# A transformer trunk on one core: weight loads queued five chunks ahead, three quarters of the residual transposed by DMA, last stores on one queue

## The chip, the cores and the metric

The kernel runs on one core of a Trainium2 chip. The core has TensorE (matrix products), VectorE (DVE), ScalarE (ACT) and GpSimd (POOL) as computing engines, SyncE (SP), which here only issues DMAs, and 16 DMA engines that move data between HBM and the on-chip memory SBUF. TensorE writes to PSUM, a small accumulation memory. Each engine takes its instructions in order; semaphores order the engines among each other. The metric is the device time of one execution in microseconds, as the median of several runs. Before the change it is 821.35 us (three runs, 820.9 to 821.37).

## The reference, cut to what matters

A trunk of two pre-norm residual layers over 256 tokens of width 2048, in float32, and a last RMS norm:

```python
def reference(x, norm_g, final_g, w_in_even, w_out_even, rpb_b, w_in_odd, w_out_odd, sinks_c, qnorm_d, knorm_d):
    h = x
    for layer in range(DEPTH):              # 2
        y = rms_norm(h, norm_g[layer])
        if layer % 2 == 0:
            h = h + even_layer(y, w_in_even[i], w_out_even[i], rpb_b[i])
        else:
            h = h + odd_layer(y, w_in_odd[i], w_out_odd[i], sinks_c[i], qnorm_d[i], knorm_d[i])
    return rms_norm(h, final_g)
```

Each layer projects the normed input (2048 to 8192 columns in the even layer, fewer in the odd one), runs two groups of eight attention heads of width 128 on parts of the result, multiplies their outputs by a SiLU gate, and projects the 2048 columns back. The even layer has a dilated sliding-window group and a neighbourhood group with a learned position bias (`rpb_b`); the odd layer has windowed grouped-query attention with sinks and dense attention with normed and rotated queries and keys. The weights, some 140 MB, are used once each.

## The kernel before, in words

**Products in three parts.** Every float32 matrix is split into a high half (rounded to the type that TensorE multiplies fast, `F32R`) and a low half (the rest). A product is then high x high + high x low + low x high. `split` (L89) makes the halves of data: ACT casts or scales into `hi`, DVE subtracts into `lo`.

**Weights in chunks.** All weights come as 274 chunks of 128 x 1024 words (512 KB) in the order of the list `plan`. A `Weights` object (L54) loads a chunk into one of five `wraw` buffers through SP (L65, or `pinned` for the first eight), casts it into one of three `whi` buffers on ACT (L69) and subtracts into `wlo` on DVE (L70). `weights()` (L78) keeps three such objects made and hands out the oldest. So in the program's text the load stands just ahead of its cast; the planner of the framework, which orders each engine's instructions by a simulated time, may issue it earlier. `pinned` (L85) and `keep_in_program_order` tie an instruction behind the one that the program put before it on the same engine; what isn't tied may slip past others.

**The steps.** `by_feature` (L258) takes four chunks for 256 features (16 products a chunk), `by_token` (L277) eight chunks for 512 columns (12 products a chunk of 512 columns). After each chunk `step()` (L216) does one piece of the side work: one eviction of a finished accumulator (`evac`), one piece of `post`, and one piece of an attention (`bg`). An attention of two heads (`attend`, L406) goes through logits, probabilities, transposition, splits and the weighing of the values, a piece per chunk.

**The transposition in the attention** (L458 to L475) uses no TensorE: POOL copies the words of the probabilities into two planes of 16-bit halves (L463), two DMA transposes, `pinned` on SP through L87, turn them, and POOL joins the halves to words again (L474).

**The bias of a neighbourhood head** (`bias_rpb`, L388) is loaded by four small DMAs from a table in HBM into a single buffer `rpb`, and POOL subtracts it from a mask (L403). Two heads are loaded when a query projection is evicted, which occurs four times, in the third and fourth unit of the even layer.

**Between the layers.** `project_out("even", next_input)` multiplies the gated outputs (`mh`, `ml`) by the output weights for four blocks `n` of 512 columns of h: blocks 0 and 1 together in 16 chunks, then block 2 in 8, then block 3 in 8. When a block is complete, `add_h` (L539) adds it to h on DVE and `next_input` (L654) makes the odd layer's input of it: eight TensorE transposes against `ident` into PSUM (`ps_ht`, L660), four splits with the norm's gain (L95, L96), and the square sums for the norm on ACT.

**Start and end.** While the first eight chunks are multiplied, `opening(j)` loads the four blocks of x into h (`load_h`, for j = 4 to 7), for the square sums of the first norm. At the end, block 3 of the odd output is finished one token tile after the other: its last four weight chunks are made early, in the room of the input tiles X (`beside`, L755), and `finish` (L798) scales h on DVE or ACT and stores it through SP, two of the last six stores through ACT's queue (L806, L807).

Of the kernel before, what the change touches and what calls it, by code (L numbers as in the profile page):

```python
# [9 lines left out]
F32 = mybir.dt.float32  # L10
F32R = mybir.dt.float32r
# [7 lines left out]
P = 128  # L19
# [11 lines left out]
WARM = 15  # L31
AHEAD = 2
RPB_R, RPB_C = 15, 31


@with_exitstack
def encoder(ctx, tc, a, out):
# [3 lines left out]
    big = pool("big", 1)  # L41
    wp = pool("wp", 5)
    hp = pool("hp", 3)
# [10 lines left out]
    class Weights:  # L54


        def __init__(self, src, hi=None, lo=None, x=None):
            raw = wp.tile([P, 1024], F32, tag="wraw", name="wraw")
            self.hi = hi or hp.tile([P, 1024], F32R, tag="whi", name="whi")
            self.lo = lo or hp.tile([P, 1024], F32R, tag="wlo", name="wlo")  # L60
            cuts = KK if x in (0, 1) else 1
            cols = [slice(i * 1024 // cuts, (i + 1) * 1024 // cuts) for i in range(cuts)]
            for i, c in enumerate(cols):
                load = nc.sync.dma_start if x is None else pinned
                load(raw[:, c], src[:, c])  # L65
                if x is not None and i == 0:
                    pinned(xraw[x], a["xt"][x].rearrange("p (k t) -> p k t", k=KK))
            for i, c in enumerate(cols):
                nc.scalar.copy(self.hi[:, c], raw[:, c])  # L69
                nc.vector.tensor_sub(self.lo[:, c], raw[:, c], self.hi[:, c].bitcast(F32))  # L70
                if x is not None:
                    for m in (i,) if cuts > 1 else range(KK):
# [15 lines left out]

    def split(hi, lo, src, scale=None):  # L89

        if scale is None:
            nc.scalar.copy(hi, src)
# [123 lines left out]
    def step():  # L216

        advance(evac)
        advance(post)
        attention()  # L220

    def attention():
# [13 lines left out]
    def drain():  # L236
        while evac or post or bg:
            step()

    def need(pr):  # L240
# [310 lines left out]
    def out_plan(kind):  # L551
        plan.extend((a["w_out_" + kind][n][pr], None) for n, pr in out_order(kind))

# [6 lines left out]
    for u in range(4):  # L560
        for pr, kind in even_order(u):
            if kind == "v":
                plan.extend((a["even_t"][u][j], None if u else j) for j in range(8))
            else:
                plan.extend((a["even_f"][2 * u + pr]["qkg".index(kind)][j], None) for j in range(4))
    out_plan("even")
    for t, fs in ((0, ()), (1, (10, 11)), (2, (12, 13))):
        plan.extend((a["odd_t"][t][j], None) for j in range(8))
        plan.extend((a["odd_f"][f][j], None) for f in fs for j in range(4))
    plan.extend((a["odd_f"][f][j], None) for f in (0, 1, 2, 6, 3, 7, 4, 8, 5, 9) for j in range(4))  # L570
    out_plan("odd")
# [174 lines left out]
    def beside(n, i):  # L746
# [5 lines left out]
        if n == 2 and i % 2:  # L752
            j = i // 2
            room = X[j].rearrange("p k c t -> p (k c t)")
            final.append(Weights(a["w_out_odd"][NN - 1][late[j]], room[:, :1024], room[:, 1024:]))  # L755
        if (n, i) in ((2, 4), (2, 6), (3, 1)):
# [41 lines left out]
    def finish(n, t, r, cols=full, scalar=False):  # L798
# [8 lines left out]
        pin(queue.dma_start(out[t * P : (t + 1) * P, n * 512 + cols.start : n * 512 + cols.stop], y))  # L807

# [107 lines left out]
```

## Time and profile before

| | |
|---|---|
| median of three runs | 821.35 us |
| the profiled execution | 820.54 us, its span 818.8 us |
| TensorE (PE) busy | 808.6 us, 99% of the span |
| VectorE (DVE) / ScalarE (ACT) / GpSimd (POOL) busy | 576.1 / 447.3 / 110.6 us |
| moved by DMA | 166.91 MB, mean 204 GB/s |
| mean granted TensorE clock | 0.996 |

The span runs from the first to the last instruction of the profile. A row of a group gives line, engine, operation, output<-input, shape, count, then busy time in us, mean ns of one, and the idle time of the engine ahead of it with what ended it. A row of a timeline gives start and length in us. A row of who waited for whom gives total us, times, and the longest. A row of windows gives the window, its length, and the busy us of each engine with its instruction count in brackets, then the clock, the DMA engines' busy share and GB/s. SPq and ACTq are the issuing queues of SP and ACT.

### The profile page before, as it was taken

The numbers are of one execution on the slowest core, as the hardware profiler recorded it, in microseconds if no ns is written. First come the engines' busy times: TensorE is split into PE (matmuls) and PEld (weight loads), VectorE is DVE, ScalarE is ACT, GpSimd is POOL, SyncE is SP. The second block draws the span as 40 slices with busy tenths as digits, with TensorE's granted clock in tenths as the row PEclk, the third lists the DMA queues.
The fourth block names the chain that finished last, engine by engine and source line by source line (L and its number), as shares of the span: only waits on it lengthen the run. The fifth ranks groups of instructions, "written<-read, shape, count | busy, mean of one in ns | idle before, by whom it ended". The sixth has DMA issues, their size and how long they took to land.

```text
span 818.8 us, 11775 instructions
## 1 busy us (share of the span) xinstructions
PE 808.6 (99%) x4317; PEld 695.1 (85%) x4317; DVE 576.1 (70%) x856; ACT 447.3 (55%) x712; POOL 110.6 (14%) x88
## 2 busy tenths in 40 slices
PE   9999999999999999999999999999999999999995
PEld 7888888888888888888888888888899888888884
DVE  6677675677857886587655577685987777775763
ACT  7745454554545554455445544657666665664651
POOL 0002020021302140050200000002112222221000
PEclk9999999999999999999999999999999999999998
DMA  8956765575755766565654555556577775777532
GB/s 336 354 210 209 271 213 177 208 213 168 233 182 171 241 173 220 203 194 197 213 177 172 186 186 172 200 192 198 161 183 226 224 222 184 227 197 225 209 126 104
DMA packets 90682, 166.91 MB, mean 204 GB/s; under 512 B 48960, under 2 KB 50112, under 8 KB 90560
## 3 DMA queue, kind: packets, MB, share of 16 engines
q1 hardware_dynamic: 90192, 165.61, 62.5%
q8 instruction: 34, 0.56, 0.3%
q10 hardware_dynamic: 432, 0.54, 0.2%
q14 instruction: 24, 0.20, 0.1%
HBM read 155.64 MB, written 3.05 MB: 194 GB/s over the span
## 4 chain that ended last, share of the span: by engine, by line
PE 98%; DMA 0%; ACT 0%; DVE 0%; issue 0%; ACTq 0%; DVEq 0%
PE ps_f L267 34%; PE ps_f L271 17%; PE ps_t L102 14%; PE ps_t L103 14%; PE ps_t L104 14%; PE ps_s L103 1%; PE ps_s L104 1%; PE ps_s L102 1%; PE ps_out L103 1%; PE ps_out L102 1%; PE ps_out L104 1%; PE ps_ht L660 0%; DMA wraw<-in_even_t 0%; PE ps_tr L372 0%; ACT h L803 0%; ACT whi L69 0%
## 5 line engine op out<-in xcount | busy, mean ns | idle before, releaser
L70 DVE TENSOR_TENSOR wlo<-wraw,whi 128x1024 fp32r<-128x1024 f32 (+1 forms) x270 | 344.4, 1276 | 187.8 <-ACT whi L69 187.3
L69 ACT CAST whi<-wraw 128x1024 fp32r<-128x1024 f32 (+1 forms) x270 | 281.9, 1044 | 300.9 <-PE ps_t L104 130.7
L267 PE MATMUL ps_f<-x,whi 128*128 128x512 f32 x1184 | 372.3, 396 | 0.0
L271 PEld LDWEIGHTS ps_f<-x,wlo 128*128 128x128 f32 x1184 | 222.4, 188 | 52.9 <-DVE wlo L70 0.7
L271 PE MATMUL ps_f<-x,wlo 128*128 128x256 f32 x1184 | 233.0, 278 | 0.0
L267 PEld LDWEIGHTS ps_f<-x,whi 128*128 128x128 f32 x1184 | 180.9, 189 | 0.5
L102 PE MATMUL ps_t<-whi,x 128*128 128x512 f32 (+1 forms) x256 | 96.8, 381 | 0.3 <-ACT x L95 0.3
L103 PE MATMUL ps_t<-wlo,x 128*128 128x512 f32 (+1 forms) x256 | 96.4, 379 | 0.0
L104 PE MATMUL ps_t<-whi,x 128*128 128x512 f32 (+1 forms) x256 | 96.1, 377 | 0.0
L463 POOL COPY ph<-pr 128x1024 uint16<-128x1024 uint16 x32 | 39.5, 1233 | 418.1 <-ACT pr L453 252.0
L102 PE MATMUL ps_t<-whi,mh 128*128 128x512 f32 x240 | 93.8, 391 | 0.0
L103 PE MATMUL ps_t<-wlo,mh 128*128 128x512 f32 x240 | 93.7, 391 | 0.0
L104 PE MATMUL ps_t<-whi,ml 128*128 128x512 f32 x240 | 93.6, 390 | 0.0
L104 PEld LDWEIGHTS ps_t<-whi,x 128*128 128x128 f32 x256 | 48.5, 189 | 9.0
L102 PEld LDWEIGHTS ps_t<-whi,x 128*128 128x128 f32 x256 | 48.5, 189 | 9.0 <-ACT x L95 0.6
L474 POOL COPY pt<-pa 128x1024 uint16<-128x1024 uint16 x32 | 50.4, 1576 | 37.5 <-DMA pa<-ph 37.2
L103 PEld LDWEIGHTS ps_t<-wlo,x 128*128 128x128 f32 x256 | 48.6, 190 | 8.2
L104 PEld LDWEIGHTS ps_t<-whi,ml 128*128 128x128 f32 x240 | 45.1, 188 | 9.3
L103 PEld LDWEIGHTS ps_t<-wlo,mh 128*128 128x128 f32 x240 | 45.1, 188 | 8.9
L102 PEld LDWEIGHTS ps_t<-whi,mh 128*128 128x128 f32 x240 | 45.1, 188 | 8.9
L445 ACT ACTIVATE pr<-lg,mn 128x256 f32<-128x256 f32 (+1 forms) x48 | 24.0, 501 | 16.5 <-POOL ph L463 8.9
L403 POOL TENSOR_TENSOR bias<-maskB,rpb 128x512 f32<-128x512 f32 x8 | 12.5, 1567 | 138.5 <-DMA rpb<-rows 138.5
(129 smaller groups left out, 664.4 us busy)
## 6 DMA issues: line engine op xcount, KB each, us to landing
wraw<-in_even_f SPq DMA_DIRECT2D x96, 512.0 KB, 3.5
wraw<-in_odd_f SPq DMA_DIRECT2D x56, 512.0 KB, 3.7
wraw<-in_w_out_even SPq DMA_DIRECT2D x32, 512.0 KB, 3.3
wraw<-in_w_out_odd SPq DMA_DIRECT2D x32, 512.0 KB, 4.3
wraw<-in_even_t SPq DMA_DIRECT2D x30, 512.0 KB, 4.3
wraw<-in_odd_t SPq DMA_DIRECT2D x24, 512.0 KB, 3.2
xraw<-in_xt SPq DMA_DIRECT2D x8, 256.0 KB, 7.0
h<-in_x SPq DMA_DIRECT2D x4, 512.0 KB, 8.6
```

The lines of the kernel that those rows point to most:

```text
L69: nc.scalar.copy(self.hi[:, c], raw[:, c])
L70: nc.vector.tensor_sub(self.lo[:, c], raw[:, c], self.hi[:, c].bitcast(F32))
L102: nc.tensor.matmul(dst, lh, rh, start=first, stop=False, skip_group_check=True)
L103: nc.tensor.matmul(dst, lh, rl, start=False, stop=False, skip_group_check=True)
L104: nc.tensor.matmul(dst, ll, rh, start=False, stop=last, skip_group_check=True)
L267: nc.tensor.matmul(acc[:, f, :], w.hi[:, c], xx[k], start=k == 0, stop=False, skip_group_check=True)
L271: nc.tensor.matmul(acc[:, f, :S], w.lo[:, c], xh[k], start=False, stop=k == KC - 1, skip_group_check=True)
L403: nc.gpsimd.tensor_tensor(b, maskB.unsqueeze(1).to_broadcast([P, 2, S]), raw, op=ALU.subtract)
L445: nc.scalar.activation(p[:, t, :W], lg[:, t, :W], AF.Exp, bias=mn[:, t : t + 1], scale=-1.0, accum_out=den[:, t : t + 1],)
L463: nc.gpsimd.tensor_copy(halves, words)
L474: nc.gpsimd.tensor_copy(words.bitcast(U16).rearrange("p c (q s) -> p s c q", s=2), st[i])
```

## The change

- `Weights` is parted: the constructor only loads, always `pinned`; `prepare()` casts and subtracts. `load_ahead()` keeps up to five loaded chunks that aren't prepared, and is called before each preparation and once more before a chunk is handed out. The four early chunks of the last block come through the same plan, with the X tiles as their halves, and `beside` takes them by `weights()`.
- `load_h(n)` is called at j = 1 to 4.
- `next_input` no longer uses TensorE for blocks 0, 1 and 2. Per half block (`c`) a generator `turned_input` is queued in `turns`: POOL copy into 16-bit planes; two DMA transposes; an empty step; POOL copy back to words (in the single `rpb` buffer); two splits, whose ACT part is tied in program order; an empty step. `turning()`, called at the end of each `step()`, moves each generator on by one step, the next one only when the one before it has done three. Block 3 keeps the TensorE transposes.
- `finish` always stores through SP, and the order and cut of the last token tile's stores differ: block 0 in two halves, block 1, block 2, block 3 whole.

```diff
+RAW = 5
...
-    wp = pool("wp", 5)
+    wp = pool("wp", RAW)
...
         def __init__(self, src, hi=None, lo=None, x=None):
-            raw = wp.tile([P, 1024], F32, tag="wraw", name="wraw")
-            self.hi = hi or hp.tile([P, 1024], F32R, tag="whi", name="whi")
-            self.lo = lo or hp.tile([P, 1024], F32R, tag="wlo", name="wlo")
+            self.raw = wp.tile([P, 1024], F32, tag="wraw", name="wraw")
+            self.hi, self.lo, self.x = hi, lo, x
             cuts = KK if x in (0, 1) else 1
-            cols = [slice(i * 1024 // cuts, (i + 1) * 1024 // cuts) for i in range(cuts)]
-            for i, c in enumerate(cols):
-                load = nc.sync.dma_start if x is None else pinned
-                load(raw[:, c], src[:, c])
+            self.cols = [slice(i * 1024 // cuts, (i + 1) * 1024 // cuts) for i in range(cuts)]
+            for i, c in enumerate(self.cols):
+                pinned(self.raw[:, c], src[:, c])
                 if x is not None and i == 0:
                     pinned(xraw[x], a["xt"][x].rearrange("p (k t) -> p k t", k=KK))
-            for i, c in enumerate(cols):
+
+        def prepare(self):
+            raw, x = self.raw, self.x
+            if self.hi is None:
+                self.hi = hp.tile([P, 1024], F32R, tag="whi", name="whi")
+                self.lo = hp.tile([P, 1024], F32R, tag="wlo", name="wlo")
+            for i, c in enumerate(self.cols):
                 nc.scalar.copy(self.hi[:, c], raw[:, c])
...
-    plan, ready = [], []
-
-    def weights(ahead=AHEAD):
-
-        while plan and len(ready) <= ahead:
-            src, x = plan.pop(0)
-            ready.append(Weights(src, x=x))
+    plan, loaded, ready = [], [], []
+
+    def load_ahead():
+        while plan and len(loaded) < RAW:
+            loaded.append(Weights(*plan.pop(0)))
+
+    def weights():
+
+        while (plan or loaded) and len(ready) <= AHEAD:
+            load_ahead()
+            ready.append(loaded.pop(0))
+            ready[-1].prepare()
+        load_ahead()
         return ready.pop(0)
...
-    def split(hi, lo, src, scale=None):
+    def split(hi, lo, src, scale=None, kept=lambda x: x):
...
-            nc.scalar.mul(hi, src, scale)
+            kept(nc.scalar.mul(hi, src, scale))
...
     def step():
...
         attention()
+        turning()
...
+    turns = []
+
+    def turning():
+
+        for i, t in enumerate(list(turns)):
+            if i and steps[id(turns[i - 1])] < 3:
+                break
+            steps[id(t)] += 1
+            next(t)
+        if turns and steps[id(turns[0])] == 6:
+            turns.pop(0)
...
     def out_plan(kind):
-        plan.extend((a["w_out_" + kind][n][pr], None) for n, pr in out_order(kind))
+        for n, pr in out_order(kind):
+            plan.append((a["w_out_" + kind][n][pr],))
+            if (kind, n) == ("odd", 2) and pr in ORDER[kind][1::2]:
+                j = ORDER[kind].index(pr) // 2
+                room = X[j].rearrange("p k c t -> p (k c t)")
+                plan.append((a["w_out_odd"][NN - 1][ORDER[kind][4 + j]], room[:, :1024], room[:, 1024:]))
...
-        if j > 3:
-            load_h(j - 4)
+        if 0 < j < 5:
+            load_h(j - 1)
...
+    def turned_input(n, c):
+
+        halves = tp.tile([P, 2, 2, S], U16, tag="tmp2", name="hh")
+        across = tp.tile([P, 2, 2, S], U16, tag="pr", name="ha")
+        cols = h[n][:, :, c * S : (c + 1) * S].bitcast(U16)
+        nc.gpsimd.tensor_copy(halves, cols.rearrange("p t (k s) -> p t s k", s=2))
+        yield
+        for t in range(2):
+            pinned(
+                across[:, :, :, t * P : (t + 1) * P].rearrange("p s c q -> p (s c) q"),
+                halves[:, t].rearrange("p s k -> p (s k)"), transpose=True,
+            )
+        yield
+        yield
+        words = tp.tile([P, 2, S], F32, tag="rpb", name="hw", bufs=1)
+        nc.gpsimd.tensor_copy(words.bitcast(U16).rearrange("p c (q s) -> p s c q", s=2), across)
+        yield
+        for i in range(2):
+            k = 4 * n + 2 * c + i
+            split(xh[k], xl[k], words[:, i, :], gcol[:, KC + k : KC + k + 1], tc.keep_in_program_order)
+        yield
+        yield
+
     def next_input(n):
 
+        if n < NN - 1:
+            for c in range(2):
+                turns.append(turned_input(n, c))
+                steps[id(turns[-1])] = 0
+            square_sums(parts1, n)
+            return
         for c in range(2):
...
-            final.append(Weights(a["w_out_odd"][NN - 1][late[j]], room[:, :1024], room[:, 1024:]))
+            final.append(weights())
...
-        queue = nc.scalar if scalar and t else nc.sync
-        pin(queue.dma_start(out[t * P : (t + 1) * P, n * 512 + cols.start : n * 512 + cols.stop], y))
+        pin(nc.sync.dma_start(out[t * P : (t + 1) * P, n * 512 + cols.start : n * 512 + cols.stop], y))
...
     finish(0, 1, r, halves[0])
+    finish(0, 1, r, halves[1])
     finish(1, 1, r, scalar=True)
-    finish(0, 1, r, halves[1])
     finish(2, 1, r, scalar=True)
-    finish(3, 1, r, halves[0])
-    finish(3, 1, r, halves[1])
+    finish(3, 1, r)
```

More of the change, by code (lines that the diff above doesn't have):

```diff
@@ L238, in drain @@
             step()
+        while turns:
+            turning()
+    turns = []
[7 more added lines that the diff above has]
+            turns.pop(0)
+    steps = {}
     def need(pr):
@@ L562, in encoder @@
             if kind == "v":
-                plan.extend((a["even_t"][u][j], None if u else j) for j in range(8))
+                plan.extend((a["even_t"][u][j], None, None, None if u else j) for j in range(8))
             else:
-                plan.extend((a["even_f"][2 * u + pr]["qkg".index(kind)][j], None) for j in range(4))
+                plan.extend((a["even_f"][2 * u + pr]["qkg".index(kind)][j],) for j in range(4))
     out_plan("even")
     for t, fs in ((0, ()), (1, (10, 11)), (2, (12, 13))):
-        plan.extend((a["odd_t"][t][j], None) for j in range(8))
-        plan.extend((a["odd_f"][f][j], None) for f in fs for j in range(4))
-    plan.extend((a["odd_f"][f][j], None) for f in (0, 1, 2, 6, 3, 7, 4, 8, 5, 9) for j in range(4))
+        plan.extend((a["odd_t"][t][j],) for j in range(8))
+        plan.extend((a["odd_f"][f][j],) for f in fs for j in range(4))
+    plan.extend((a["odd_f"][f][j],) for f in (0, 1, 2, 6, 3, 7, 4, 8, 5, 9) for j in range(4))
     out_plan("odd")
```

6 lines of the change are left out of this document (2 added, 4 removed).

## The prediction, written before the result was known

> **What bounds the kernel now.** I read the page first (busy times, then the chain of waits), then who waited for whom on TensorE, then the timelines of the stretches that the diff touches.
>
> ```profile
> span 818.8 us, 11775 instructions
> PE 808.6 (99%) x4317; PEld 695.1 (85%) x4317; DVE 576.1 (70%) x856; ACT 447.3 (55%) x712; POOL 110.6 (14%) x88
> PE 98%; DMA 0%; ACT 0%; DVE 0%; issue 0%; ACTq 0%; DVEq 0%
> PEld ps_f L271 <- DVE wlo L70: 0.7, 2, 0.4
> 805.00:818.80 13.80, 5.12 (x29) 4.30 (x27) 6.97 (x21) 3.99 (x9) 0.00 (x0) 0.78 0.43 154
> ```
>
> The chain that ended last lies on TensorE for 98% of the span. Its longest wait for weights sums to 0.7 us. The span less the busy time is 818.8 - 808.6 = 10.2 us, of which 13.80 - 5.12 = 8.7 us lie in the last window, behind the last product (the row's first columns: length, then busy TensorE), and nearly all the rest ahead of the first. So time is won in three ways only: fewer instructions on TensorE, an earlier start, a shorter tail. It is lost in one way: something TensorE needs comes late. The profiled execution took 820.54 us, 1.74 more than its span; the median of the runs is 821.35, so I work out a difference on the profiled one and take it from the median.
>
> **Part 1: 24 of 32 transposes leave TensorE.** This is the block for one of the four 512-column blocks of h, between products:
>
> ```profile
> 425.87 0.39 PE L104 MATMUL ps_t<-whi,ml 128*128 128x512 f32 x1
> 426.09 0.39 PE L102 MATMUL ps_t<-whi,mh 128*128 128x512 f32 x1
> 426.36 0.44 PE L660 MATMUL ps_ht<-ident,h 128*128 128x128 f32 x2
> 426.55 0.49 PE L103 MATMUL ps_t<-wlo,mh 128*128 128x512 f32 x1
> 426.88 0.40 PE L104 MATMUL ps_t<-whi,ml 128*128 128x512 f32 x1
> 427.12 0.82 PE L660 MATMUL ps_ht<-ident,h 128*128 128x128 f32 x6
> 427.69 0.48 PE L102 MATMUL ps_t<-whi,mh 128*128 128x512 f32 x1
> 428.00 0.40 PE L103 MATMUL ps_t<-wlo,mh 128*128 128x512 f32 x1
> ```
>
> Undisturbed products start 0.22 to 0.23 us apart (425.87, 426.09). From 426.09 to 428.00 four of them start (426.09, 426.55, 426.88, 427.69), which would take 4 x 0.227 = 0.91 us and take 1.91: eight transposes cost 1.0 us. Three of the four blocks change: **-3.0 us**. TensorE takes its instructions in order and never waits here, so this comes off the end in full, unless the replacement makes it wait.
>
> The replacement, per half block: one POOL copy into halves, two DMA transposes, one POOL copy back to words, then the same two splits on ACT and DVE. The attention does just that with its probabilities, on tiles of the same size:
>
> ```profile
> L463 POOL COPY ph<-pr 128x1024 uint16<-128x1024 uint16 x32 | 39.5, 1233 | 418.1 <-ACT pr L453 252.0
> L474 POOL COPY pt<-pa 128x1024 uint16<-128x1024 uint16 x32 | 50.4, 1576 | 37.5 <-DMA pa<-ph 37.2
> L87 SPq DMA_TRANSPOSE pa<-ph x64: 1188/1252/2134, 70.1 to 739.8; - x64
> 425.00:475.00 50.00, 50.00 (x233) 40.97 (x232) 29.73 (x37) 26.37 (x42) 0.00 (x0) 1.00 0.51 180
> ```
>
> Six halves: POOL 6 x (1.23 + 1.58) = 16.9 us, in a stretch (last row: 425 to 475 us, columns TensorE, weight load, DVE, ACT, POOL, clock, DMA share, GB/s) where POOL does nothing; SP 12 x 1.25 = 15.0 us of issuing in 50 us, beside some 18 weight loads. I cost both at nothing. The cover on POOL is the order in `turning`: six steps per half, one step per product chunk, the next half starting when the one before it is three steps in. Counting chunks, the third block's last splits come in the last chunk but one of the projection, four chunks or more (11 us) ahead of the first product of the odd layer that reads them. Were that cover gone, each late half would hold TensorE for the rest of its chain, for the copy back (1.6 us) and the splits.
>
> On SP the transposes wait for the POOL copy, and behind them queue the weight loads, for which ACT's casts wait; the margin there is worked out in the second part. The splits themselves stay: the same two instructions on tiles of the same size, read from SBUF where they were read from PSUM; on ACT and DVE I cost the difference at nothing, since neither sets the pace there (29.73 and 26.37 us busy of 50).
>
> **Part 2: loads five chunks ahead.**
>
> ```profile
> SPq L65 <- DVE wlo L70: 443.9, 201, 5.8
> wraw<-in_w_out_even SPq DMA_DIRECT2D x32, 512.0 KB, 3.3
> ```
>
> SP spent 443.9 us waiting for a subtraction to give back one of the five raw buffers: the loads already go out as early as five buffers allow. So in steady state this edit is worth **0**. What it changes is the order on SP: `pinned` loads stand strictly where the program has them, and so do the transposes, bias loads and table loads between them, which until now could slip past. The margin: a buffer comes back every chunk (12 products, 2.7 us), so a load is issued some 13.6 us ahead of the buffer's next return, lands 3.3 us later, and the cast and subtraction take the last 2.3: about 8 us between landing and cast. SP may be held 8 us in one piece before a cast is late.
>
> At the start the loads of h move behind the weights:
>
> ```profile
> 9.62 0.39 SPq L87 DMA_DIRECT2D h<-in_x  x1
> ...
> 15.48 0.38 SPq L87 DMA_DIRECT2D h<-in_x  x1
> 16.20 0.33 SPq L65 DMA_DIRECT2D wraw<-in_even_f  x1
> 5.09:28.00 22.91, 22.91 (x96) 18.88 (x97) 16.33 (x27) 15.75 (x28) 0.00 (x0) 1.00 1.02 392
> 26.28 1.05 ACT L69 CAST whi<-wraw 128x1024 fp32r<-128x1024 f32 x1 [2.23 <-DMA wraw<-in_even_f]
> 28.05 0.61 PE L267 MATMUL ps_f<-x,whi 128*128 128x512 f32 x2
> 28.98 0.63 PE L267 MATMUL ps_f<-x,whi 128*128 128x512 f32 x2
> 29.68 0.63 PE L267 MATMUL ps_f<-x,whi 128*128 128x512 f32 x2
> ```
>
> The transfers run at 392 GB/s there, so one load of 512 KB takes 1.3 us. Three loads of h (9.62 to 15.48) stand ahead of the first feature-major chunk and only one will; that chunk lands about 2.6 us earlier. Its cast is late now: the group at 28.05 takes 0.93 us to the next one, where the following takes 0.70. **-0.2 us**; bounds 0 and -0.4. The last block of h comes about 2.6 us later, covered by the three chunks before its square sum is due. The first product doesn't move: the queue ahead of it keeps its order.
>
> The four early weights of the last block now come through the plan, so the ready-ahead of two counts them. Their casts stand at 765 to 784 us and their products begin after the last ordinary chunk, so nothing there is near TensorE: **0**.
>
> **Part 3: the last stores on one queue.**
>
> ```profile
> L807 SPq DMA_DIRECT2D out<-h x4: 348/411/448, 807.8 to 809.2; - x4
> DMA to landing us min/median/max: 2.0/2.5/2.7
> L807 SPq DMA_DIRECT2D out<-h x4: 332/352/392, 812.7 to 814.4; - x4
> L807 ACTq DMA_DIRECT2D out<-h x2: 367/368/369, 813.1 to 814.3; - x2
> DMA to landing us min/median/max: 1.9/2.8/3.3
> 812.35 0.72 ACT L803 ACTIVATE h<-h,rc_r 128x512 f32<-128x512 f32 x1 [0.79 <-DVE rc_r L795]
> ```
>
> The first two rows are the four stores of the first token tile: 256 KB each, one queue, last landing at 809.2 + 2.7 = 811.9. The next three are the six of the second tile on two queues, the same 1 MB: last landing at 814.4 + 3.3 = 817.7, and the end follows it. After the change five stores follow each other on SP. The issue pitch is 0.41 us, so from 812.7 the fifth goes out at 814.4 again; ACT's two scalings, no longer parted by an issue on ACT, end by 812.35 + 2 x 0.72 = 813.8, so the data is there. If it lands as late as the first group's, the end is at 817.1: **-0.6 us**; if as late as now, 0. I take -0.6, from the nearest row, one queue with full-width stores; range 0 to -0.8. The Trainium skill, in "DMA: Bandwidth & Descriptors", section "Issuing engines are not separate DMA queues", speaks against it: transfers from all queues share the same DMA engines, and a second issuing engine only saves issue time. By that rule merging the queues wins nothing, and the forecast would be 0.6 us higher; the two groups (4.1 us for 1 MB on one queue, 5.0 on two) lean the other way.
>
> **The sum.** -3.0 - 0.2 - 0.6 = -3.8 us: 820.54 becomes 816.7 in a profiled execution, and the median of 821.35 becomes **817.5 us**. With the small terms at their bounds, 816.9 to 818.4.
>
> **Rivals.** *First: SP's strict order starves an attention head (slower).* At four places the bias of two neighbourhood heads is loaded through a single buffer while another head pair is being transposed. Here it is in the third unit of the even layer:
>
> ```profile
> 204.69 1.91 SPq L87 DMA_DIRECT2D rpb<-rows  x3
> 206.69 2.55 SPq L87 DMA_TRANSPOSE pa<-ph  x2
> 210.60 2.34 POOL L474 COPY pt<-pa 128x1024 uint16<-128x1024 uint16 x1 [0.57 <-DMA pa<-ph]
> 222.67 0.28 PE L102 MATMUL ps_out<-pth,vh 128*128 128x256 f32 x1
> ```
>
> These loads and transposes hold SP up to 209.2 already. In program order the load that waits for the next subtraction (about 208) would come first, then both heads' four table loads (8 x 0.6 us, with a landing and a POOL subtraction of 1.3 to 2.2 us between them), then the second pair of transposes, at about 218 in place of 206.7. They land at 221.7; the copy (1.4 to 2.3), the cast and the subtraction follow, to about 224.5, where TensorE wants the result at 222.67. That is 2 us, four times, 8 us in all: 821.35 - 3.8 + 8 = 825.5. For it: the queue. Against it: the planner orders TensorE too, and can put a weight chunk ahead of the late product, as it put whole products between the transposes at 426; then nothing is lost. It decides from transposes that land after about 219. Chance 0.12.
>
> *Second: one late low half in the odd layer takes a part back.*
>
> ```profile
> 594.13 1.21 DVE L70 TENSOR_TENSOR wlo<-wraw,whi 128x1024 fp32r<-128x1024 f32 x1
> 595.40 0.50 PE L271 MATMUL ps_f<-x,wlo 128*128 128x256 f32 x2
> 570.00:620.00 50.00, 50.00 (x324) 45.24 (x323) 45.75 (x87) 32.85 (x68) 10.99 (x8) 1.00 0.61 173
> ```
>
> DVE is 92% busy there, and a subtraction ends at 595.34 for a product at 595.40. A new order that puts one or two passes of 1.2 us ahead of it costs TensorE as much: 818.7 to 819.9. Chance 0.20.
>
> *Third: the change doesn't shorten anything,* because the halves turned by DMA come late to the odd layer or the loads in the projection do: about 821. The 8 us and 11 us above speak against it. Chance 0.08.
>
> **How the numbers follow.** The forecast has 0.60. A measurement of this kernel can tell about 0.2% (1.6 us) from no change, so faster means under 819.7. The forecast lies wholly there, the second rival for 0.13 of its 0.20: faster 0.73. Same: 0.07 of the second, 0.07 of the third, 0.02 of the first: 0.16. Slower: the rest, 0.11. The low end of the range, 816.6, is the forecast with each small term at its best and 0.3 for the spread of runs; the high end, 820.8, takes in the second rival and half of the third. The likeliest case's own range is 816.7 to 818.5.
>
> **What would show it.** Right: eight `ps_ht` transposes left, near 472; POOL busy for about 17 us between 425 and 475; TensorE without a wait between the first product and the last, the last about 3.2 us earlier; the group after 28 us at its 0.70 pitch; stores on SP alone, the end 8.1 us behind the last product where it is 8.7. Wrong: a row in which TensorE waits for the probabilities' low half near 223, 281, 317 or 376, or for `wlo` near 595; more than 12 new transposes on SP with casts waiting for `wraw`.

## The result: 1.2% slower, and the profile after

The median is 832.06 us (826.66 to 833.77, four runs) against 821.12 us (820.82 to 821.37, four runs) beside it: a ratio of 1.0123, 95% interval 1.0088 to 1.0158. The forecast was 817.5 us. The profiled execution took 831.4 us, with a span of 829.6.

The page of the changed kernel: its first line, TensorE's busy time, and the chain that ended last.

```profile
span 829.6 us, 11768 instructions
PE 811.9 (98%) x4293; PEld 695.5 (84%) x4293; DVE 579.8 (70%) x855; ACT 447.7 (54%) x712; POOL 133.5 (16%) x100
PE 91%; DMA 2%; DVE 2%; POOL 1%; ACT 1%; SPq 1%; issue 0%; ACTq 0%; POOLq 0%; DVEq 0%
```

TensorE has 24 instructions fewer (4293) and is busy 3.3 us *longer*; the chain leaves it for DMA, DVE, POOL, ACT and SP, which hardly appeared in it before. Who TensorE waited for in the changed kernel (total us, times, longest):

```profile
PE ps_out L113 <- ACT pth L510: 6.8, 4, 2.2
...
PE ps_out L114 <- DVE ptl L511: 0.7, 2, 0.3
PE ps_bc L204 <- DVE rb L203: 0.4, 1, 0.4
```

Four waits for the cast of the transposed probabilities, 6.8 us, and behind two of them another for the subtraction that makes their low half. The same chunk of weights can be found in both traces, so the start of its first product shows where the changed kernel falls behind (my subtraction, us, after less before):

```
chunk                         20     72     76     96    108    128    144    152    160    204    last product   end
after less before          +0.06  +0.06  +2.32  +6.18 +10.02 +14.39 +13.36 +12.30 +11.26 +11.60     +11.60    +10.84
```

Four steps of 2.26, 3.86, 3.84 and 4.37 us (14.3 in all) at the third and fourth unit of the even layer; three gains of 1.0 us at the three blocks turned by DMA (-3.1); a loss of 0.4 near 606 us; an end that is 0.76 shorter. The sum is +10.84, the difference of the spans.

The first of the four steps on SP's queue, before and then after:

```profile
192.67 2.65 SPq L87 DMA_DIRECT2D rpb<-rows  x4
...
200.14 0.58 SPq L87 DMA_DIRECT2D rpb<-rows  x1
201.75 2.89 SPq L87 DMA_TRANSPOSE pa<-ph  x2
```

```profile
205.32 2.50 SPq L98 DMA_TRANSPOSE pa<-ph  x2
207.92 0.52 SPq L98 DMA_DIRECT2D wraw<-in_even_t  x1
208.49 9.62 SPq L98 DMA_DIRECT2D rpb<-rows  x8
218.49 2.52 SPq L98 DMA_TRANSPOSE pa<-ph  x2
```

Before, five of the eight table loads were out ahead of the first pair of transposes, and the second pair went out at 206.69. After, all eight stand between the pairs, 9.62 us with the wait for the single `rpb` buffer, and the second pair goes out at 218.49. What follows from it on the other engines:

```profile
222.36 1.44 POOL L502 COPY pt<-pa 128x1024 uint16<-128x1024 uint16 x1 [0.83 <-DMA pa<-ph]
222.51 0.39 PE L115 MATMUL ps_t<-whi,x 128*128 128x512 f32 x1
...
223.84 0.62 ACT L510 CAST pth<-pt 128x512 fp32r<-128x512 f32 x1 [2.79 <-POOL pt L502]
...
224.51 0.39 PE L113 MATMUL ps_out<-pth,vh 128*128 128x256 f32 x1 [1.61 <-ACT pth L510]
```

The product due at 222.74 (0.23 behind the last one, of 222.51) starts at 224.51; that is 1.77 of the step's 2.26 us, and more than half of the rest is the wait for the low half. The other three places cost 1.6 to 2.1 us more than this one. These windows show why (window, its length, then busy us of TensorE, weight load, DVE, ACT, POOL with instruction counts; clock, DMA share, GB/s):

```profile
220.68:224.10 3.42, 2.22 (x10) 1.50 (x8) 3.42 (x2) 0.63 (x2) 2.30 (x2) 1.00 0.69 210
224.10:227.51 3.41, 2.90 (x14) 2.32 (x15) 2.26 (x4) 2.03 (x3) 0.00 (x0) 1.00 1.00 386
```

```profile
282.12:285.54 3.42, 1.64 (x9) 1.10 (x7) 3.19 (x3) 0.62 (x1) 1.63 (x1) 1.00 0.88 296
285.54:288.95 3.41, 3.40 (x12) 3.01 (x13) 1.93 (x3) 1.66 (x2) 0.00 (x0) 0.50 1.00 366
```

Behind the second stall the granted clock is 0.50 for 3.41 us: half the products fit, which costs up to half of 3.41, or 1.7 us. The third and the fourth place have such a stretch too (from 326.50 and 387.94), the first has none.

### The profile page after: what moved, and what is told of

Its sections match the earlier page's. It is cut to its first block, busy times and chain, and to the rows that moved or that the text cites. A ratio compares the mean times of both kernels' runs of the same rounds, so it can differ in the third digit from the quotient of the medians.

```text
span 829.6 us, 11768 instructions
## 1 busy us (share of the span) xinstructions
PE 811.9 (98%) x4293; PEld 695.5 (84%) x4293; DVE 579.8 (70%) x855; ACT 447.7 (54%) x712; POOL 133.5 (16%) x100
## 4 chain that ended last, share of the span: by engine, by line
PE 91%; DMA 2%; DVE 2%; POOL 1%; ACT 1%; SPq 1%; issue 0%; ACTq 0%; POOLq 0%; DVEq 0%
PE ps_f L295 31%; PE ps_f L299 15%; PE ps_t L114 13%; PE ps_t L115 13%; PE ps_t L113 13%; DVE wlo L75 1%; PE ps_out L114 1%; PE ps_s L114 1%; PE ps_s L115 1%; PE ps_s L113 1%; DMA pa<-ph 1%; PE ps_out L115 1%; SPq L98 1%; POOL pt L502 1%; PE ps_out L113 1%; DMA wraw<-in_even_t 1%
## 5 line engine op out<-in xcount | busy, mean ns | idle before, releaser
L502 POOL COPY pt<-pa 128x1024 uint16<-128x1024 uint16 x32 | 55.3, 1729 | 29.3 <-DMA pa<-ph 29.2
L510 ACT CAST pth<-pt 128x512 fp32r<-128x512 f32 x32 | 19.5, 617 | 31.4 <-POOL pt L502 31.3
L511 DVE TENSOR_TENSOR ptl<-pt,pth 128x512 fp32r<-128x512 f32 x32 | 25.3, 799 | 10.0 <-ACT pth L510 10.0
```

Source lines behind the costliest of these rows:

```text
L502: nc.gpsimd.tensor_copy(words.bitcast(U16).rearrange("p c (q s) -> p s c q", s=2), st[i])
L510: tc.keep_in_program_order(nc.scalar.copy(hi, st[i]))
L511: nc.vector.tensor_sub(lo, st[i], hi.bitcast(F32))
```

## The experiments

Theory A, as I began: the loads are now tied, and that holds the table loads behind them. Theory B: the queue has no share, and the planner puts the late product earlier on TensorE, because loads and casts are now written apart. The refined form of A is A2: it is the *place* of the load ahead of them in the written order, a load for seven chunks on, which has to wait for its buffer. Rivals: that any tie does it, that Part 1 has a share, that the stalls come from something else than SP's order. In the results, the stall is the sum of the four steps worked out from chunk starts as above. The start of the whole differs by up to 2 us between profiled executions, at the first few chunks and in kernels with the same start too, so places are compared and not spans.

**Loads no longer tied** (the changed kernel; five ahead stays).

```diff
-                pinned(self.raw[:, c], src[:, c])
+                load = nc.sync.dma_start if x is None else pinned
+                load(self.raw[:, c], src[:, c])
```

> The changed kernel, but weight loads after the first eight chunks are no longer tied to program order on SP; all else stays (five ahead, residual by DMA, last stores on one queue). Theory A (SP's strict order): in the changed kernel a load that waits for a subtraction, then eight bias-table loads with a POOL subtraction between them, stand ahead of the second pair of DMA transposes, so the pair goes out at 218.5 us and TensorE waits 2.2 to 2.7 us at four places, with 3.4 us of half clock behind three of them. With free loads the queue gets the order of the kernel before: no wait over 0.3 us at the four places, time 821.1 - 3.1 (transposes) - 0.8 (tail) = 817.2 us, between 816.6 and 818.2. Theory B (the planner places the late product earlier on TensorE because casts and loads are now traced apart, not because of the queue): the waits stay, 825 us or more.

Measured: 828.88 us (826.52 to 831.7), ratio to before 1.0101 (1.0071 to 1.0131). SP's timeline and TensorE's waits in this kernel:

```profile
207.06 2.50 SPq L99 DMA_TRANSPOSE pa<-ph  x2
...
210.22 2.65 SPq L99 DMA_DIRECT2D rpb<-rows  x4
...
220.09 2.60 SPq L99 DMA_TRANSPOSE pa<-ph  x2
```

```profile
PE ps_out L114 <- ACT pth L511: 5.8, 4, 2.0
```

The tables still go out between the pairs without the ties, and the stalls stay (1.75, 1.66, 1.49 and 3.77 us, the last with a half-clock stretch). Theory A falls in its first form; theory B isn't met by this run, but by the next two, which keep loads and casts apart and have no stall.

**The table loads one step later** (the changed kernel; a step between the query's eviction and the loads).

```diff
+            yield
             st["bias"] = [bias_table(a["bias_a"][x]) if p < 4 else bias_rpb(x) for x in heads]
```

> The changed kernel, loads still tied; only the loading of the two heads' bias is put one step (one chunk) later than the eviction of the queries, so that in program order the second pair of transposes of the attention under way comes ahead of the eight bias-table loads. Theory A: the pair goes out at about 208.5 instead of 218.5 us, no wait over 0.3 us at the four places, 817.2 us (816.6 to 818.2). If tying the loads is harmful by itself, wherever the bias loads stand, or theory B holds (the planner's order on TensorE), the waits stay and the time is 825 us or more.

Measured: 819.36 us (817.76 to 822.17, nine runs), ratio 0.9976 (0.9964 to 0.9987). No stall at the four places in the profile. SP in this kernel:

```profile
211.62 2.61 SPq L98 DMA_TRANSPOSE pa<-ph  x2
...
214.89 7.15 SPq L98 DMA_DIRECT2D rpb<-rows  x5
```

The second pair now goes ahead of the tables. One line that touches neither the weight loads nor the transposes takes all 14 us of stalls away. The pair went out 3.1 us later than the 208.5 expected, and the median missed the expected range by 1.2 us: the profile is of the fastest of the nine runs, and what slows the others isn't shown.

**A second room for the table** (the changed kernel; the second head's table goes into another buffer, so that its four loads don't wait for POOL).

```diff
-        raw = tp.tile([P, 2, S], F32, tag="rpb", name="rpb", bufs=1)
+        raw = tp.tile([P, 2, S], F32, name="rpb", **(dict(tag="tmp2") if head % 2 else dict(tag="rpb", bufs=1)))
```

> The changed kernel, loads still tied and the order of the queue as it is; the second head's bias table gets a buffer of its own, so its four loads no longer wait for POOL's subtraction of the first head. Theory A, with the single buffer as the larger part of the delay: the eight loads end about 213.5 us instead of 218.1, the transposes land at about 218.6, the copy, cast and subtraction end about 221.5, TensorE wants them at 222.5: the four waits shrink from 2.2 to 2.7 us to under 0.6 us each, no half clock, 817.2 to 819.5 us. If the load that waits for a subtraction is the larger part: waits of over 1.5 us stay, 823 us or more.

Measured: 817.94 us (817.19 to 818.09), ratio 0.9958 (0.9943 to 0.9973), no stall. SP in this kernel:

```profile
209.52 5.36 SPq L98 DMA_DIRECT2D rpb<-rows  x8
214.98 2.54 SPq L98 DMA_TRANSPOSE pa<-ph  x2
```

The order is that of the changed kernel; the block of tables between the pairs is 5.36 us long in place of 9.62, and that is enough.

**Part 1 alone** (the kernel before, with `turned_input` and `turning` as in the change).

> The kernel before with the residual's part alone: three blocks turned by DMA in the queued steps; loads made as before, last stores on two queues. By the changed kernel's own chunk starts, the three blocks save 3.1 us: 818.0 us, between 817.5 and 818.6. Rival (the loads in the projection come late behind the transposes when the loads aren't queued ahead in order): 819.5 to 821.

Measured: 817.72 us (816.65 to 818.12), ratio 0.9955 (0.994 to 0.997). The three blocks bring 1.01, 1.06 and 1.04 us, 3.1 together; no stall at the attention; 0.4 lost at chunks 200 to 204, as in the changed kernel.

**The ties alone** (the kernel before, all its weight loads tied; none ahead).

```diff
-                load = nc.sync.dma_start if x is None else pinned
-                load(raw[:, c], src[:, c])
+                pinned(raw[:, c], src[:, c])
```

> The kernel before, with one edit: its weight loads are tied into the written order as the changed kernel's are; no load ahead of the subtractions, no turning by DMA, the old stores. Theory A2 (what holds the table loads back is that the load traced just ahead of them belongs to a chunk whose buffer comes free only five chunks on; in the kernel before that load was issued long ago, so that nothing holds the tables): no stall at the attention heads, the second pair of transposes issued between 205 and 209 us as before, 820.5 to 822. Rival (tying the loads is itself what orders the tables behind the transposes): stalls of 1.5 to 4 us at the four places, 826 to 832.

Measured: 872.71 us (871.77 to 873.71), ratio 1.0633 (1.0617 to 1.0649). Neither theory had this. SP's timeline, then the waits of SP and of TensorE:

```profile
202.54 2.70 SPq L86 DMA_TRANSPOSE pa<-ph  x2
...
205.91 9.01 SPq L86 DMA_DIRECT2D rpb<-rows  x8
214.97 2.60 SPq L86 DMA_TRANSPOSE pa<-ph  x2
217.61 0.58 SPq L86 DMA_DIRECT2D wraw<-in_even_f  x1
```

```profile
SPq L86 <- POOL ph L462: 177.4, 24, 18.0
```

```profile
PE ps_f L266 <- ACT whi L68: 30.6, 7, 7.3
```

Here the tables do stand behind the first pair, as the rival had it, so ties alone bring that order as well: A2's expectation of no stall, with the second pair issued between 205 and 209, falls, and so does its reading that nothing but the far load holds the tables. The price is another one: SP stands up to 18.0 us for POOL's halves with the weight loads tied behind, the next weights go out at 217.61, and TensorE waits 7.3 us for their cast. So the ties need the loads ahead: without them they cost over 50 us. The loads ahead don't need the ties, since the untied kernel above was no slower than the changed one.

**Four ahead in place of five** (the changed kernel).

```diff
-        while plan and len(loaded) < RAW:
+        while plan and len(loaded) < RAW - 1:
```

> The changed kernel with the loads four chunks ahead of the subtraction in place of five. Theory A2: the load traced ahead of the table loads waits for a subtraction that is one chunk (2.7 us) earlier, so the tables of the first place are issued about 2.7 us earlier than 208.5 us, the second pair of transposes at 214.5 to 216 us, which leaves 0 to 0.5 us of stall at each of the four places; without half-clock stretches 817 to 819.5. Rival (any load ahead of its cast does it, whatever the number): stalls as in the changed kernel, transposes at 218 us or later, 825 or more.

Measured: 818.16 us (817.59 to 819.52), ratio 0.9968 (0.9957 to 0.9979), no stall. SP in this kernel:

```profile
206.70 9.12 SPq L98 DMA_DIRECT2D rpb<-rows  x8
215.86 2.87 SPq L98 DMA_TRANSPOSE pa<-ph  x2
```

The tables start 1.8 us earlier than in the changed kernel (2.7 were expected), the second pair at 215.86 (214.5 to 216 expected), and the median lies in the expected range.

One reading fits the orders of all these kernels. The bias loads are `pinned`, which ties them behind what the program put just before them on SP, and that is a weight load. Where that load goes, the tables follow. In the kernel before it goes out early, and so do they (192.67, straight behind two weight loads). With the ties alone it stands behind the first pair, and they do too (205.91). With five ahead, tied or not, it waits for its buffer (given back at 207.70 in the changed kernel), and they start at 208.49. No run moved that one load alone, so this stays a reading.

**Part 2 without Part 1** (the changed kernel, all four blocks turned by TensorE again: `if n < 0` for `if n < NN - 1` in `next_input`).

> The changed kernel with all four blocks of h turned by TensorE again: Parts 2 and 3 of the change without Part 1. Theory A2 (the stalls come from the load of a chunk seven ahead in the written order, and Part 1 has no share in them): a stall of 1.5 to 2.5 us at each of the four places of the even layer, the second pair of transposes at 218 to 220 us, and the changed kernel's time plus the 3.1 us that Part 1 wins: 829 to 837, about 835. Rival (Part 1's generators share in the stalls): under 829.

Measured: 834.08 us (831.92 to 838.1), ratio 1.0154 (1.0137 to 1.0171). Stalls at all four places (4.4, 4.0, 3.8, 3.9 us), each followed by a half-clock stretch. SP in this kernel:

```profile
210.04 9.61 SPq L98 DMA_DIRECT2D rpb<-rows  x8
220.03 2.68 SPq L98 DMA_TRANSPOSE pa<-ph  x2
```

Part 1 has no share in the stalls.

**The tail alone** (the kernel before; the last stores as in the change: all on one queue, the last tile's fourth block whole, its first block's halves one behind the other).

```diff
-        queue = nc.scalar if scalar and t else nc.sync
-        pin(queue.dma_start(
+        pin(nc.sync.dma_start(
...
     finish(0, 1, r, halves[0])
+    finish(0, 1, r, halves[1])
     finish(1, 1, r, scalar=True)
-    finish(0, 1, r, halves[1])
     finish(2, 1, r, scalar=True)
-    finish(3, 1, r, halves[0])
-    finish(3, 1, r, halves[1])
+    finish(3, 1, r)
```

> The kernel before, with the last stores alone changed as in the change: all on one queue, the last tile stored whole. If the 0.76 us that the changed kernel's end was shorter come from where the 8 KB instruction fetch falls among the last stores and not from the queue: within 0.3 us of before, and the time from the last product to the end follows the fetch (8.0 to 8.2 us without a fetch after the last product or with an early one, 8.7 to 8.9 us with one some 5 to 6.5 us after it). If merging the queues brings it: 0.5 to 0.9 us faster.

Measured: 821.54 us (820.8 to 822.21, eleven runs), ratio 1.0007 (0.9998 to 1.0016). Merging the queues wins nothing. The median is 0.55 us above the 820.99 beside it, where at most 0.3 was expected. The time from the last product to the end goes with an instruction fetch of 8 KB (queue 14 in the page's numbering) and where it falls behind the last product (times from the start of that product; the last column is where the last packet of a store ends):

```
kernel                     queues   fetch begins   last product to end   last store packet
before                     two      +5.47 us       8.91 us               7.31 us
Part 1 alone               two      none           8.00 us               6.83 us
added waits (below)        two      +2.16 us       8.02 us               6.83 us
after                      one      +1.77 us       8.15 us               6.90 us
loads not tied             one      none           8.14 us               6.90 us
four ahead                 one      +4.49 us       8.76 us               7.44 us
tables one step later      one      +6.34 us       8.78 us               7.42 us
the tail alone             one      +4.84 us       9.22 us               7.67 us
Part 2 without Part 1      one      +8.68 us       8.86 us               6.90 us
```

In the four kernels with a fetch between 4.5 and 6.3 us, the last store's packets end 0.4 to 0.8 us later than in those with an early fetch or none, and the end comes at 8.76 to 9.22 us in place of 8.00 to 8.15, whichever queues they store on. Without a late fetch, one queue is no faster than two (8.14 and 8.15 against 8.00 and 8.02). Part 2 without Part 1 doesn't fit: its fetch begins only when the stores are through, and why its end is late stays open. No run moved the fetch by itself.

**Added waits** (Part 1 alone, and work added that the reference doesn't have: at every fifth feature-major chunk TensorE waits for a chain of small copies on POOL).

```diff
+LENGTHS = (2, 4, 6, 9)
...
+        z = ps_at.tile([P, 4], F32, tag="at", name="ps_gap")
+        tc.keep_in_program_order(nc.tensor.matmul(z[:, :2], ident, ones[:, :2], start=True, stop=True))
+        t = sm.tile([P, 2], F32, tag="gap", name="gap")
+        nc.vector.tensor_copy(t, z[:, :2])
+        for _ in range(LENGTHS[chunk[0] // 5 % len(LENGTHS)]):
+            u = sm.tile([P, 2], F32, tag="gap", name="gap")
+            nc.gpsimd.tensor_copy(u, t)
+            t = u
+        tc.keep_in_program_order(nc.tensor.matmul(z[:, 2:], ident, t, start=True, stop=True))
```

> The kernel before with the turning by DMA alone, and work added: at every fifth feature-major chunk from the fifteenth on, TensorE waits for a chain of 2, 4, 6 or 9 small copies on GpSimd, in turn. It asks from which length of a wait on the half clock follows. Theory C (a wait of about 2 us or more is followed by a stretch of 3.4 us at a granted clock of 0.5): the half clock follows the long chains and not the shortest, and each such stretch costs about 1.7 us beside the wait. Rival (the half clock falls where it falls, whatever the waits): it shows as often after the short chains, or not at all.

The one run took 922.16 us. The waits didn't come out by the length of the chain, since POOL and DVE had other work ahead of the copies (waits from 0.2 to 5.6 us), so the question as asked stays without an answer. But every half-clock stretch of the run begins a whole multiple of 3.413 us behind the first one. So I laid that grid over the trace, and took from each window the time not covered by products at their undisturbed pitch (0.227 us for 512 columns, 0.113 for 256). Windows of this kernel, in pairs:

```profile
166.51:169.92 3.41, 2.73 (x19) 2.21 (x17) 2.57 (x6) 1.65 (x3) 1.68 (x5) 1.00 0.59 208
169.92:173.33 3.41, 2.14 (x12) 1.92 (x13) 1.32 (x6) 0.60 (x2) 2.01 (x6) 1.00 0.49 159
186.99:190.40 3.41, 1.64 (x11) 1.31 (x10) 0.86 (x1) 0.00 (x0) 2.32 (x3) 1.00 1.23 263
190.40:193.81 3.41, 3.41 (x13) 2.93 (x12) 0.00 (x0) 0.00 (x0) 1.32 (x1) 0.50 0.57 154
```

The wait near 170 us is the longer one (2.35 us from product to product), but the grid parts it, 1.03 and 1.48 us of idle time in two windows, and the clock stays at 1.00. The one near 188 us (2.05 us) lies in one window with 2.15 us idle, and the next runs at 0.50.

**The changed kernel once more**, to try that rule on stalls that it wasn't made from.

> The changed kernel once more, unchanged, for the rule read from the runs with added waits. Theory D: the granted clock is set for windows of 3.413 us on a fixed grid; a window in which TensorE idles for more than about 2.1 us is followed by one at half clock, one with less by none, and a stall that the grid parts between two windows goes free. Then every half-clock window of this run lies behind a window with over 2.1 us of idle time, and the span is 824.5 to 825.5 plus 1.7 us for each such window between the first product and the last. Rival (each stall of over 2 us is followed by the half clock wherever it falls): all four stalls or those of the greatest length, whatever the grid.

Measured: 829.1 us, span 827.3. Two of its stalls on the grid:

```profile
222.38:225.79 3.41, 2.48 (x11) 1.69 (x9) 3.27 (x2) 0.62 (x2) 2.77 (x2) 1.00 0.60 176
225.79:229.20 3.41, 2.45 (x12) 1.95 (x13) 2.27 (x4) 1.88 (x3) 0.14 (x1) 1.00 0.99 344
...
382.81:386.22 3.41, 1.72 (x11) 1.34 (x9) 2.03 (x2) 0.17 (x1) 3.21 (x2) 1.00 0.80 225
386.22:389.63 3.41, 2.57 (x15) 2.19 (x16) 1.98 (x3) 2.05 (x3) 0.00 (x0) 1.00 1.00 396
```

All four stalls are there (10.1 us), the grid parts each of them in two, the most idle window has 1.86 us, and no product runs at half clock. The rule held. The span, expected at 824.5 to 825.5, is off: this execution began 2.0 us later.

## Why the prediction was wrong

**Part 2 failed, at "in steady state this edit is worth 0".** The working found the strict order on SP and set against it a margin of "about 8 us" that a weight load can be late. That margin was right for the casts: after the change TensorE has no wait of note for weights in the even layer. But it was worked out for one customer of the queue, the casts. The other customer, the second pair of transposes, had no such margin. The first rival had exactly this and its prices hold: second pair "at about 218" (218.49), the result "to about 224.5" (224.51), four places, 2 us each (2.26 at the undisturbed one, 10.1 for the four in the changed kernel's second profile). The sign of being wrong came too, a wait for the probabilities (for their high half first). The rival got a chance of 0.12 on one sentence, that the planner "can put a weight chunk ahead of the late product". It didn't: the last product ahead of the wait starts at 222.51, the next at 224.51. The row that the prediction had for it, products between the transposes near 426, showed products between instructions that weren't late, and nothing in the profile showed one put ahead of a late product. The order of TensorE is written before the run, and a planner that believes the data will be there may leave no room. Which time its plan had for the second pair wasn't looked into.

The boundary fits too: "it decides from transposes that land after about 219". The kernels whose second pair was issued by 215.86 (landed by 219.97) had no stall for the probabilities, those issued at 218.49 or later (landed from 222.22 on) had four; no run lies between. Three unlike edits (tables later, tables shorter, tables earlier) take the stalls away, which shows the cause to be the table loads between the pairs. What puts the tables behind the first pair isn't one thing: with the ties alone it comes about, and with five loads ahead without ties too. The reading behind "Four ahead in place of five" covers both, untested.

**What the rival lacked is the clock.** It came to 825.5 us; the median is 832.06. The stalls without a half clock are 10.1 us rather than 8 (the changed kernel's second profile), and the three half-clock stretches of the first profile bring the other 4.3 of its 14.3 us. This also gives a reason for the wide spread: the mean granted clock of the four runs was 0.998 at 826.66 us, 0.991 at 831.4 and at 832.71, and 0.989 at 833.77. The Trainium skill, in "TensorE: Matmul & The Clock Gate", section "What's actually happening", describes a free-running activity window of 3413 ns and a half-rate clock after an idle one; the grid and the 0.50 agree.

**Part 1 was right**: -3.1 us for -3.0. Eight `ps_ht` transposes are left, and the cover on POOL held; here the group of transposes in the changed kernel (count, then ns least/median/most, first and last start), and the window that answers to 425 to 464 us of before:

```profile
L722 PE MATMUL ps_ht<-ident,h x8: 270/272/328, 487.0 to 488.3; 128*128 128x128 f32 x8
```

```profile
436.00:475.00 39.00, 39.00 (x174) 32.30 (x173) 29.03 (x29) 22.22 (x34) 15.09 (x10) 1.00 0.91 218
```

TensorE is busy for all 39.00 us, with ten of POOL's twelve copies (15.09 us) beside it; 16.9 were expected for twelve.

**The start: -0.2 became a loss of some 0.6.** The first group of the first feature-major chunk came to its pitch (27.77 to 28.46, 0.69 us). That wasn't the edit: Part 1 alone (29.21 to 29.90) and the tail alone (29.01 to 29.69) load x in the old order and have the same pitch, so the 0.93 belonged to the one profile that the prediction was read from. Then TensorE waits for the norm's factors. From chunk 10 to chunk 20 the changed kernel (in both profiles) and four of the five others with its loads lose 0.6 us against the kernel before (0.35 with four ahead); the three that keep the old order of x and of the loads lose nothing. The row of the last load of x, before and after, and the changed kernel's rows:

```profile
17.50 0.38 SPq L87 DMA_DIRECT2D h<-in_x  x1
```

```profile
19.15 0.38 SPq L98 DMA_DIRECT2D h<-in_x  x1
```

```profile
27.77 0.62 PE L295 MATMUL ps_f<-x,whi 128*128 128x512 f32 x2
...
28.46 0.63 PE L295 MATMUL ps_f<-x,whi 128*128 128x512 f32 x2
...
44.85 0.48 DVE L203 TENSOR_SCALAR rb<-ones,rstd 128x128 f32<-128x128 f32 x2
...
45.28 0.30 PE L204 MATMUL ps_bc<-ident,rb 128*128 128x128 f32 x1 [0.41 <-DVE rb L203]
```

The last block of x goes out 1.65 us later and lands 2.4 us later (27.55, then 29.95), near the "about 2.6" of the working, and "covered by the three chunks" held: its square sums on ACT start at 37.04 and 39.59. The loss comes behind that. The last square sum stood at 37.86 before, and between the norm's small steps on DVE two subtractions of weights now stand where one stood, so `rb`, made from 43.16 on before, is made from 44.85 on. Why the planner orders them so stays open, and no run parts the order of x from that of the loads.

**The tail: right in size by luck, wrong in reason.** -0.6 was forecast for merging the queues, -0.76 measured, and the tail alone shows that merging wins nothing (ratio 1.0007). What differs in the profiles is the fetch. The two groups of stores that I compared differed in that as well, and I read the difference as one of queues. The rule of the Trainium skill quoted there, that issuing engines aren't separate queues, agrees with the run.

**The second rival's place** took 0.4 us in every kernel with Part 1, far under its 1.2 to 2.4. The kernel before there, then the changed one:

```profile
596.12 0.69 DVE L365 TENSOR_TENSOR ru<-ru,rw 128x512 f32<-128x512 f32 x1
```

```profile
607.14 1.38 POOL L502 COPY pt<-pa 128x1024 uint16<-128x1024 uint16 x1 [2.54 <-DMA pa<-ph]
607.34 1.67 DVE L393 TENSOR_TENSOR ru<-ru,rw 128x512 f32<-128x512 f32 x1
608.93 1.21 DVE L75 TENSOR_TENSOR wlo<-wraw,whi 128x1024 fp32r<-128x1024 f32 x1
610.20 0.30 PEld L299 LDWEIGHTS ps_f<-x,wlo 128*128 128x128 f32 x2 [0.45 <-DVE wlo L75]
```

The product at 595.40, which the rival named, isn't the one that came late (it stands at 606.62 in the changed kernel, behind the same wait): the loss falls 3.6 us further, at 610.20. There DVE's `ru` takes 1.67 us beside a copy on POOL where it took 0.69 without one, the subtraction behind it ends late, and the weight load for its product waits. So the rival had the engine right (DVE at 92%), but an instruction became longer where it had expected a pass put in between.

**The range.** "With the small terms at their bounds, 816.9" doesn't follow from its terms: -3.0 - 0.4 - 0.8 = -4.2 gives 817.15, so the range began 0.25 us too low, which decides nothing here.

**What stands of the change.** Part 1 alone (817.72 us) or the whole change with a second room for the table (817.94) are both faster than the kernel before by 0.4%, which is nearly all that the forecast had.

## What to carry to other kernels

When an in-order DMA queue gets a stricter order, work out the lateness of *every* transfer on it, not only of the stream that was edited: here the weights had 8 us to spare and two small transposes had none. A rival that is worked out to the tenth of a microsecond may be dismissed only by a row that shows the same case; here the row showed another. Where a pipeline on TensorE has no slack, price a stall of 2 us at up to 4, because the clock may follow it.

## What the runs showed of the hardware

**The half clock hangs on a grid, not on the length of a wait.** Over six profiles (after, once more, loads not tied, Part 2 alone, ties alone, added waits), of the windows of 3.413 us at full clock and with over 0.3 us of idle time, 26 had 2.15 us or more idle and all 26 were followed by a window at 0.50; 69 had 2.02 us or less and none was. Counting each small product by its columns moves the two bounds to 2.21 and 2.05 us; they stay apart. So the bound lies near 2.1 us of 3.41. A stall of 2.2 to 2.5 us costs nothing more or up to 1.7 us more by where the grid falls in that execution. The Trainium skill, in "TensorE: Matmul & The Clock Gate", section "Why this matters for your kernels", advises no idle gaps of over some 3 us; here 2.1 us in one window were enough.

**An instruction fetch of 8 KB among the last stores,** 4.5 to 6.3 us behind the last product, goes with an end that is 0.6 to 1.2 us later in four kernels, by the table above.
